# Part of the expert weights as plain float32, the rest split on VectorE alone, the gate inside a one-hot operand

## The chip, the cores and the metric

The kernel runs on one core of a Trainium2 chip, whose core has five engines: TensorE (PE, with its weight loads shown as PEld), VectorE (DVE), ScalarE (ACT), GpSimd (POOL) and SyncE (SP), which issues most of the transfers. The metric is the device time of one launch in microseconds, lower is better; it is taken as the median of several runs.

## What is computed

Two transformer blocks follow each other (256 tokens, width 1024, float32 throughout), then a third stage with a latent and a context stream in two layers. The change touches one thing alone, the expert layer of the latent stream, once in each of the two layers. For a token row `x` with norm and modulation already applied it is

```python
qry = (xb @ w_query).reshape(P, 8, 2, 128)
s = jnp.einsum('phcd,hckd->phck', qry, sub_keys)          # 128 keys for each half
top_s, top_i = lax.top_k(s, 16)
cand_s = top_s[..., 0, :, None] + top_s[..., 1, None, :]  # 16 x 16 pairs
cand_i = top_i[..., 0, :, None] * 128 + top_i[..., 1, None, :]
best_s, pos = lax.top_k(cand_s.reshape(...), 16)
idx = jnp.take_along_axis(cand_i.reshape(...), pos, axis=-1)
gate = jax.nn.softmax(best_s, axis=-1)
act = gelu(jnp.einsum('pd,phkd->phk', xb, u_tab[idx]))
out = jnp.einsum('phk,phkd->pd', gate * act, v_tab[idx])
```

There are 128 x 128 experts, so each of the two tables `u_tab` and `v_tab` has 16384 rows of 1024, and a token picks 8 x 16 of them.

## The kernel before

The latent stream's expert layer is done densely (`class Dense`, driven by `lat_peer`): instead of gathering rows, all 16384 experts are multiplied with all tokens, in 128 chunks of 128 experts, and the gates, which are zero for experts not picked, are multiplied in between. Layer 0 does all 256 tokens so (T = 256); in layer 1 the first 48 tokens go by gathers (`Few`) and 208 are dense (T = 208). A float32 product is made of three products in a reduced format, fp32r: `split` takes a weight tile of 128 x 512 (256 KB), casts it to its upper 12 bits `sh` (line 509 on VectorE, 511 on ScalarE), subtracts that from the tile to get the lower part `sl` (line 513, on VectorE or GpSimd), and the product is `sh*xh + sh*xl + sl*xh`, where `xh` and `xl` are the parts of the activation (`xs`, made once in `peer_in`). The pairs in the constants `SPD`, `SPT` and `SPL` say, for each tile in turn, whether VectorE casts, and whether VectorE subtracts: before, `SPT` and `SPD` (routing; second matrix) cast on ScalarE and subtract on GpSimd and VectorE by turns, and `SPL` (first matrix) does the even tiles on ScalarE and GpSimd and the odd ones on VectorE alone.

The stages of a layer, in order:

1. Routing (`prep`, `peer_route`, products by `lin_cols_split`, 16 blocks of the query weights), woven with the first chunks of the first matrix.
2. The first matrix, first 56 chunks (`up_first`): for each chunk two weight tiles `ut`, products into the PSUM bank `au`, then in layer 1 a sum `cf` (lines 1924 and 1925), then Gelu into `G`.
3. The spread (`up_spread`): for each four tokens (64 times in layer 0, 52 in layer 1) `spread` makes two one-hot operands, `ohl` over the first key (|iota - key| on ScalarE, line 1945, then Relu(1 - .), line 1946) and `ohr` over the second (an equality on VectorE, line 1947, times the gate on GpSimd, line 1949), multiplies them on TensorE into `gp`, and multiplies the result into `G` (line 1960) or copies it there (line 1962). One chunk of the first matrix goes with each spread. In `up`, the columns whose gates are already there take another product on GpSimd (line 1932).
4. The second matrix (`down`), in two halves of 512 columns, 128 chunks each: one tile `vt` a chunk, and `g`, the chunk of `G`, split into `gs` (line 1990 on ScalarE, 1991 on VectorE), products into four banks `y` that are summed over all chunks. Halves end in `finish`.

Beside all this runs another stream of work, the context's gathers (`gather_sum`: a row gather into `gv` issued on GpSimd, and a multiply-add on VectorE, 128 x 1024) and in layer 1 those of `Few`. `tick` issues a step of it after so many microseconds of TensorE's work, and places it behind the instruction `E.pin`, which `split` sets to the latest subtraction on GpSimd.

Weight tiles `ut`, `vt` and the query weights `w` come from one ring of five buffers (`UB = 5`, tag "w") and are all loaded by SyncE's queue, in the order of the program. `h` and `l` tiles have five buffers (`HB`, `VB`), `gs` four. A tile scheduler orders each engine's queue ahead of time; an engine does its queue in that order. A load waits until the last reader of the tile five before it is done:

## Time and profile before

| | |
|---|---|
| median of 3 runs | 4541.75 us (4533.81 to 4548.85) |
| span of the profiled execution | 4545.1 us, 3.35 above the median |
| granted TensorE clock, mean | 0.927 |
| busy: PE, DVE, ACT, POOL | 85%, 77%, 44%, 54% |

The stages that the change touches lie between 2309 and 3398 us (layer 0) and between 3554 and 4533 us (layer 1):

| stage | layer 0, us | length | layer 1, us | length |
|---|---|---|---|---|
| routing | 2309 to 2364 | 55 | 3554 to 3607 | 53 |
| first matrix, first 56 chunks (layer 1: 48) | 2364 to 2570 | 206 | 3607 to 3777 | 170 |
| spread, with about 63 chunks | 2570 to 2894 | 324 | 3777 to 4080 | 303 |
| last chunks of the first matrix | 2894 to 2926 | 32 | 4080 to 4142 | 62 |
| second matrix, half 0 | 2926 to 3152 | 226 | 4142 to 4344 | 202 |
| second matrix, half 1 | 3152 to 3398 | 246 | 4344 to 4533 | 189 |

Together they are 2068 us. "Busy" counts an engine's time inside instructions; for matmuls the ends are modelled, so that two that follow each other overlap, and the time of one is read from the distance between starts.

### The profile page before, as it was taken

How to read it: one execution, taken by the hardware profiler on the slowest of the kernel's cores; microseconds unless marked ns; L12 is line 12 of the kernel's file. 1: busy time of each engine (PE TensorE's matmuls, PEld its weight loads, DVE VectorE, ACT ScalarE, POOL GpSimd, SP SyncE). 2: the span in 40 equal slices, each digit the busy share in tenths (PEclk: the TensorE clock that was granted, in tenths of full speed). 3: DMA queues.
4: the chain of work that ended last, by engine and by line, in shares of the span. 5: the costliest groups of instructions: out<-in, count | busy, mean ns of one | idle time of the engine just before them, and what ended most of it. 6: DMA issues, size and time to landing. Idle time of an engine off the chain costs nothing.

```text
span 4545.1 us, 71987 instructions
## 1 busy us (share of the span) xinstructions
PE 3866.8 (85%) x24403; PEld 3111.8 (68%) x24403; DVE 3509.3 (77%) x6513; ACT 1982.2 (44%) x5025; POOL 2439.9 (54%) x2019
## 2 busy tenths in 40 slices
PE   7899878889998888897888887888887978777888
PEld 6756756377563676664588887777666777677878
DVE  4674576588565995775678899888877899998988
ACT  3224315345253443222443365455444445654555
POOL 1013235577544873113537688766554467787654
PEclk8998999999999999997899999999999988989999
DMA  5452627888878873447444754676762345557775
GB/s 173 127 187 63 235 83 267 305 288 284 304 266 296 286 257 126 123 153 240 145 150 144 244 172 159 196 229 226 247 222 68 125 144 183 181 172 231 262 234 194
DMA packets 384176, 907.74 MB, mean 200 GB/s; under 512 B 87888, under 2 KB 90000, under 8 KB 383040
## 3 DMA queue, kind: packets, MB, share of 16 engines
q1 hardware_dynamic: 270560, 553.05, 36.9%
q0 software_dynamic: 87552, 318.81, 21.2%
q10 hardware_dynamic: 25696, 31.28, 2.3%
q8 instruction: 193, 3.16, 0.3%
q14 instruction: 175, 1.43, 0.1%
HBM read 887.67 MB, written 15.32 MB: 199 GB/s over the span
## 4 chain that ended last, share of the span: by engine, by line
DVE 16%; PE 16%; DMA 7%; issue 6%; POOL 4%; ACT 1%; DVEq 0%; POOLq 0%; SPq 0%; ACTq 0%
PE y L392 8%; DVE sl L513 4%; PE au L392 3%; DMA gv<-in_peer_v_dram,ixz 2%; DVE gs L1991 2%; DVE sh L509 2%; DMA vt<-in_peer_v_dram 2%; POOL sl L513 2%; PE acs L392 2%; DMA ut<-in_peer_ut_dram 1%; DVE ohr L1947 1%; POOL ohr L1949 1%; DMA gv<-in_peer_v_dram,fix 1%; DVE G L1960 1%; DVE fg L1841 1%
## 5 line engine op out<-in xcount | busy, mean ns | idle before, releaser
L392 PE MATMUL au<-xs,sh 128*128 128x256 f32 (+1 forms) x3072 | 749.7, 329 | 73.1 <-DVE cf L1925 55.1
L392 PE MATMUL y<-gs,sh 128*128 128x512 f32 (+1 forms) x2048 | 710.1, 401 | 106.0 <-DVE gs L1991 95.8
L392 PE MATMUL au<-xs,sl 128*128 128x256 f32 (+1 forms) x2048 | 583.1, 288 | 58.5 <-DVE sl L513 39.8
L392 PEld LDWEIGHTS au<-xs,sh 128*128 128x128 f32 x3072 | 541.0, 202 | 88.4 <-DVE cf L1925 45.1
L392 PE MATMUL y<-gs,sl 128*128 128x256 f32 (+1 forms) x2048 | 554.4, 277 | 13.1 <-POOL sl L513 13.1
L513 POOL TENSOR_TENSOR sl<-vt,sh 128x512 fp32r<-128x512 f32 x256 | 388.2, 1519 | 262.6 <-ACT sh L511 221.1
L392 PEld LDWEIGHTS y<-gs,sh 128*128 128x128 f32 x2048 | 399.1, 196 | 183.7 <-DVE gs L1991 122.9
L392 PEld LDWEIGHTS au<-xs,sl 128*128 128x128 f32 x2048 | 417.9, 204 | 80.0 <-DVE sl L513 54.8
L511 ACT CAST sh<-vt 128x512 fp32r<-128x512 f32 x512 | 316.1, 619 | 347.7 <-PE y L392 165.1
L513 POOL TENSOR_TENSOR sl<-ut,sh 128x512 fp32r<-128x512 f32 x256 | 384.1, 1504 | 118.4 <-ACT sh L511 94.7
L1991 DVE TENSOR_TENSOR gs<-G,gs 128x256 fp32r<-128x256 f32 (+1 forms) x512 | 396.0, 790 | 39.3 <-ACT gs L1990 38.8
L1754 POOL DMA_INDIRECT gu<-in_peer_u_dram,ixs x256 | 289.8, 1132 | 248.8 <-DVE gu L1756 133.2
L392 PEld LDWEIGHTS y<-gs,sl 128*128 128x128 f32 x2048 | 401.5, 198 | 18.1 <-POOL sl L513 15.7
L1756 DVE SCALAR_TENSOR_TENSOR gu<-gu,h 128x1024 f32<-128x1024 f32 x256 | 361.8, 1420 | 63.7 <-DMA gu<-in_peer_u_dram,ixs 62.1
L392 PE MATMUL acs<-xs,sh 128*128 128x256 f32 (+1 forms) x1792 | 373.0, 304 | 27.5 <-ACT sh L511 15.0
L392 PE MATMUL acc<-hdn,w 128*128 128x256 f32 x1280 | 313.5, 398 | 33.3 <-DVE cvu L1269 12.6
L392 PEld LDWEIGHTS acs<-xs,sh 128*128 128x128 f32 x1792 | 299.2, 202 | 49.4 <-issue 18.6
L392 PE MATMUL acs<-xs,sl 128*128 128x256 f32 x960 | 285.3, 300 | 27.5 <-POOL sl L513 20.8
L513 DVE TENSOR_TENSOR sl<-ut,sh 128x512 fp32r<-128x512 f32 x256 | 289.7, 1133 | 15.7 <-ACT sh L511 1.6
L392 PEld LDWEIGHTS acc<-hdn,w 128*128 128x128 f32 x1280 | 245.9, 199 | 78.9 <-DVE cvu L1269 14.8
L1774 DVE SCALAR_TENSOR_TENSOR y<-gv,col,y 128x1024 f32<-128x1024 f32 x157 | 243.5, 1551 | 62.7 <-DMA gv<-in_peer_v_dram,ixz 50.1
L513 POOL TENSOR_TENSOR sl<-w,sh 128x512 fp32r<-128x512 f32 x140 | 193.3, 1384 | 143.2 <-ACT sh L511 124.0
(654 smaller groups left out, 8894.7 us busy)
## 6 DMA issues: line engine op xcount, KB each, us to landing
ut<-in_peer_ut_dram SPq DMA_DIRECT2D x512, 256.0 KB
vt<-in_peer_v_dram SPq DMA_DIRECT2D x512, 256.0 KB
w<-in_ada_w_dram SPq DMA_DIRECT2D x96, 512.0 KB
w<-in_dn_w_in_dram SPq DMA_DIRECT2D x96, 512.0 KB
w<-in_w_up_dram SPq DMA_DIRECT2D x88, 512.0 KB
wd<-in_w_down_dram SPq DMA_DIRECT2D x44, 512.0 KB
w<-in_w_in_dram SPq DMA_DIRECT2D x40, 512.0 KB
w<-in_dn_w_out_dram SPq DMA_DIRECT2D x32, 512.0 KB
```

The lines of the kernel that those rows point to most:

```text
L392: return E.nc.tensor.matmul(out, lhsT=lhsT, rhs=rhs, start=start, stop=stop)
L509: nc.vector.tensor_copy(h, src)
L511: nc.scalar.copy(h, src)
L513: ins = eng.tensor_tensor(out=l, in0=src, in1=h.bitcast(F32), op=ALU.subtract).ins
L1754: nc.gpsimd.indirect_dma_start(out=g, out_offset=None, in_=E.a["peer_u"], in_offset=bass.IndirectOffsetOnAxis(ap=ix[:, s, k:k + 1], axis=0))
L1756: nc.vector.scalar_tensor_tensor(out=g, in0=g, scalar=1.0, in1=h, op0=ALU.mult, op1=ALU.mult, accum_out=c[:, k:k + 1])
L1774: nc.vector.scalar_tensor_tensor(out=y, in0=g, scalar=c[:, k:k + 1], in1=y, op0=ALU.mult, op1=ALU.add)
L1841: nc.vector.scalar_tensor_tensor(out=g, in0=g, scalar=1.0, in1=h, op0=ALU.mult, op1=ALU.mult, accum_out=self.c[:, s, k:k + 1])
L1947: nc.vector.tensor_tensor(out=R, in0=self.iota[:, None, :].to_broadcast([128, 4, 128]), in1=col(0), op=ALU.is_equal)
L1949: nc.gpsimd.tensor_tensor(out=R, in0=R, in1=col(2), op=ALU.mult)
L1960: nc.vector.tensor_tensor(out=g[:, :, 0:m], in0=ph[:, :, 0:m], in1=g[:, :, 0:m], op=ALU.mult)
L1991: nc.vector.tensor_tensor(out=gs[:, 1], in0=g, in1=gs[:, 0].bitcast(F32), op=ALU.subtract)
```

## The change

- In both layers `SPD` is now one pair: every split tile is cast on ScalarE and subtracted on VectorE; GpSimd subtracts nothing there. `E.pin` is now the latest subtraction whichever engine does it.
- In the routing and the first matrix only the second half of the 1024 rows of the weights is split; the first half is multiplied as it is, a float32 tile times the float32 activation (`xf`), one product in place of three. `peer_in` keeps `hT` for it and splits only its second half. In `up` the split tile is loaded and multiplied first, the plain one last.
- In `down` every fourth chunk (`FD = 4`, c = 3, 7, ...) is plain: `vt` times `g` itself, without `gs`.
- The gate goes into `ohl`: in place of one Relu over 128 x 512 there are four over 128 x 128 with the gate as bias and its negative as scale (a fourth row of `sl`, made by one more ScalarE multiply). The multiply on GpSimd (line 1949) is gone.
- The multiply of `G` (line 1932) moves from GpSimd to VectorE.

Descriptions in the code's comments were taken out as well. The core of the diff, with function names in the place of line numbers:

```diff
@@ split
     eng = nc.vector if lo else nc.gpsimd
-    ins = eng.tensor_tensor(out=l, in0=src, in1=h.bitcast(F32), op=ALU.subtract).ins
-    if not lo:
-        E.pin = ins
+    E.pin = eng.tensor_tensor(out=l, in0=src, in1=h.bitcast(F32), op=ALU.subtract).ins
@@ lin_cols_split (xf: the plain activation, or None)
+    k0 = 4 if xf is not None else 0
...
-        for o in (0, 4):
+        for o in range(k0, 8, 4):
             h, l = split(E, P, ws[o // 4], o // 4)
...
+        for k in range(k0):
+            mm(E, p[:, 0:256], ws[0][:, k * 128:k * 128 + 128], xf[:, k], False, k == k0 - 1)
@@ Dense.__init__, Dense.prep
-        self.sl = P.tile([128, 3, 256], F32, name="sl")
+        self.sl = P.tile([128, 4, 256], F32, name="sl")
...
+                nc.scalar.mul(self.sl[:, 3, t * 128:t * 128 + 128], p[:, 256:384], -1.0)
@@ Dense.up
-        for o in (0, 4):
+        us = []
+        for o in (4, 0):
             ut = E.wp.tile([128, 512], F32, name="ut", tag="w")
             nc.sync.dma_start(ut, a["peer_ut"][self.i, c, :, o:o + 4].rearrange("p k e -> p (k e)"))
-            h, l = split(E, PU, ut, 2 * c + o // 4)
...
+            us.append(ut)
+        h, l = split(E, PU, us[0], 0)
+        for k in range(4):
+            e = slice(k * 128, k * 128 + 128)
+            x = self.xs[:, k, self.nb:self.nb + o1]
...
+        for k in range(4):
+            mm(E, p[:, 0:T], us[1][:, k * 128:k * 128 + 128], self.xf[:, k, self.nb:256], False, k == 3)
...
-            nc.gpsimd.tensor_tensor(out=g[:, 0:n], in0=g[:, 0:n], in1=cf[:, 0:n], op=ALU.mult)
+            nc.vector.tensor_tensor(out=g[:, 0:n], in0=g[:, 0:n], in1=cf[:, 0:n], op=ALU.mult)
@@ Dense.spread
-            nc.scalar.activation(L[:, j], self.iota, AF.Abs, bias=self.sl[:, 1, t + j:t + j + 1], scale=-1.0)
-        nc.scalar.activation(L, L, AF.Relu, scale=-1.0, bias=1.0)
-        nc.vector.tensor_tensor(out=R, in0=self.iota[:, None, :].to_broadcast([128, 4, 128]), in1=col(0),
-                                op=ALU.is_equal)
-        nc.gpsimd.tensor_tensor(out=R, in0=R, in1=col(2), op=ALU.mult)
+            nc.scalar.activation(L[:, j], self.iota, AF.Abs, bias=col(1, j), scale=-1.0)
+        for j in range(4):
+            nc.scalar.activation(L[:, j], L[:, j], AF.Relu, scale=col(3, j), bias=col(2, j))
+        nc.vector.tensor_tensor(out=R, in0=self.iota[:, None, :].to_broadcast([128, 4, 128]),
+                                in1=self.sl[:, 0, t:t + 4, None].to_broadcast([128, 4, 128]), op=ALU.is_equal)
@@ Dense.down
+            r = self.i * 16384 + c * 128
+            vt = E.wp.tile([128, 512], F32, name="vt", tag="w")
+            nc.sync.dma_start(vt, a["peer_v"][r:r + 128, n * 512:n * 512 + 512])
+            end = last and c == cs[-1]
+            if c % FD == FD - 1:
+                for k in range(4):
+                    mm(E, self.y[k][:, 0:T], vt[:, k * 128:k * 128 + 128], g, False, end)
+                continue
             gs = PV.tile([128, 2, T], F32R, name="gs", bufs=4)
@@ peer_in
-        hT = norm_T(E, PL, x, A, "hp", shift=B)
-        xs = split_x(E, P, hT, "xs", nb=nb)
+        hT = norm_T(E, P, x, A, "hp", shift=B)
+        xs = split_x(E, P, hT[:, 4:8], "xs", nb=nb)
@@ lat_peer
-                sp, E.sp = E.sp, SPT
+                E.sp = SPD
                 weave(M.prep(P, PU, nm), ups, *WP)
-                E.sp = sp
...
-                E.sp = SPD
                 M.down(PV, 0, range(128))
@@ constants
-SPD = ((0, 0), (0, 1))
-SPT = ((0, 0), (0, 1))
+SPD = ((0, 1),)
+FD = 4
```

What moves in the queues. First SyncE's queue about a third into half 0 of layer 0's second matrix: its rows are loads of `vt`, with the semaphores that each waits for (`Pool_`, `DVE_`, `PE_`: the last reader of the buffer's earlier tile). Before:

```order
L1994 DMA vt_26925<-in_peer_v_dram 128x512 [waits DMAHW1_49,Pool_49]
L1994 DMA vt_26942<-in_peer_v_dram 128x512 [waits DMAHW2_49,DVE_49]
L1994 DMA vt_26959<-in_peer_v_dram 128x512 [waits DMAHW3_49,Pool_49]
L1994 DMA vt_26979<-in_peer_v_dram 128x512 [waits DMAHW4_49,DVE_49]
L1994 DMA vt_26996<-in_peer_v_dram 128x512 [waits DMAHW5_49,Pool_49]
L1994 DMA vt_27013<-in_peer_v_dram 128x512 [waits DMAHW6_49,DVE_49]
```

and the changed kernel, at the same place:

```order
L2000 DMA vt_25239<-in_peer_v_dram 128x512 [waits DMAHW2_49,DVE_49]
L2000 DMA vt_25256<-in_peer_v_dram 128x512 [waits DMAHW3_49,DVE_49]
L2000 DMA vt_25273<-in_peer_v_dram 128x512 [waits DMAHW5_49,DMAHW0_49,DVE_49]
L2000 DMA vt_25282<-in_peer_v_dram 128x512 [waits PE_49]
L2000 DMA vt_25299<-in_peer_v_dram 128x512 [waits DMAHW6_49,DVE_49]
L2000 DMA vt_25316<-in_peer_v_dram 128x512 [waits DMAHW7_49,DVE_49]
L2000 DMA vt_25333<-in_peer_v_dram 128x512 [waits DMAHW4_49,DMAHW1_49,DVE_49]
L2000 DMA vt_25342<-in_peer_v_dram 128x512 [waits PE_49]
```

A load waited for GpSimd and VectorE by turns; now three wait for VectorE and every fourth for TensorE, which is the reader of a plain tile.

Second, VectorE's queue in the last chunks of layer 1's second matrix, where `sl` is a weight's lower part, `gs` that of `g`. Numbers rise in the order in which the program creates tiles: gs_43019 and vt_43022 before, vt_39229 and gs_39231 after, are of one chunk. Before:

```order
L513 TENSOR_TENSOR sl_43025<-vt_43022,sh_43024 128x512 [waits DMAHW1_49,PE_49,Activation_49]
L1991 TENSOR_TENSOR gs_43002<-G0_32357,gs_43002 128x208 [waits Activation_49]
L1991 TENSOR_TENSOR gs_43019<-G0_32357,gs_43019 128x208 [waits Activation_49]
L513 TENSOR_TENSOR sl_43059<-vt_43056,sh_43058 128x512 [waits DMAHW3_49,PE_49,Activation_49]
L1991 TENSOR_TENSOR gs_43036<-G0_32357,gs_43036 128x208 [waits Activation_49]
L1991 TENSOR_TENSOR gs_43053<-G0_32357,gs_43053 128x208 [waits Activation_49]
```

and the changed kernel:

```order
L513 TENSOR_TENSOR sl_39218<-vt_39212,sh_39217 128x512 [waits DMAHW5_49,PE_49,Activation_49]
L2008 TENSOR_TENSOR gs_39197<-G0_30035,gs_39197 128x208 [waits Activation_49]
L513 TENSOR_TENSOR sl_39235<-vt_39229,sh_39234 128x512 [waits DMAHW6_49,PE_49,Activation_49]
L2008 TENSOR_TENSOR gs_39214<-G0_30035,gs_39214 128x208 [waits Activation_49]
L513 TENSOR_TENSOR sl_39258<-vt_39252,sh_39257 128x512 [waits DMAHW0_49,PE_49,Activation_49]
L2008 TENSOR_TENSOR gs_39231<-G0_30035,gs_39231 128x208 [waits Activation_49]
L513 TENSOR_TENSOR sl_39275<-vt_39269,sh_39274 128x512 [waits DMAHW1_49,PE_49,Activation_49]
L2008 TENSOR_TENSOR gs_39254<-G0_30035,gs_39254 128x208 [waits Activation_49]
```

Before, one subtraction of a weight stands ahead of two of `g`. Now they alternate, and gs_39231, of the third split chunk of its group of four, stands behind sl_39258, of the first chunk of the next group; the tile of that one, vt_39252, is loaded into the buffer of the plain chunk of the group before.

Third, GpSimd's queue while the gates are spread, layer 0. Before:

```order
L1769 DMA gv_23612<-in_peer_v_dram,ixz_20755 128x1024
L1932 TENSOR_TENSOR G1_20760<-G1_20760,cf_23417 128x80
L1949 TENSOR_TENSOR ohr_23541<-ohr_23541,sl_18846 128x512
L513 TENSOR_TENSOR sl_23622<-ut_23619,sh_23621 128x512
L1932 TENSOR_TENSOR G1_20760<-G1_20760,cf_23475 128x84
L1949 TENSOR_TENSOR ohr_23599<-ohr_23599,sl_18846 128x512
L513 TENSOR_TENSOR sl_23680<-ut_23677,sh_23679 128x512
L1769 DMA gv_23713<-in_peer_v_dram,ixz_20755 128x1024
```

and the changed kernel, from the preparation of layer 0's expert layer on:

```order
L1884 IOTA iota 128x128
L1667 TENSOR_TENSOR cand<-v_18855 128x256 x8
L1694 TENSOR_TENSOR cand<-cand,fi 128x256 x16
L1667 TENSOR_TENSOR cand<-v_18856 128x256 x8
L1694 TENSOR_TENSOR cand<-cand,fi 128x256 x16
L1772 DMA gv<-in_peer_v_dram,ixz 128x1024 x121
```

The subtractions (line 513), the multiplies of `ohr` (1949) and of `G` (1932) are gone from between the gathers, and 121 gathers stand in a row.

## Rows read from the trace of the kernel before

**Rows 1.** The stretches that the change touches, cut at the stages of the two layers (the stage of each row is named in the table of times above): length, then busy time and count of each engine in the order PE, PEld, DVE, ACT, POOL, the granted TensorE clock as a share of full speed, the busy share of the DMA engines and GB/s. The line ahead gives the span.

```profile
core 0 of [0], span 4545.1 us
...
2309.00:2364.00 55.00, 54.17 (x439) 53.88 (x440) 42.30 (x191) 27.98 (x51) 29.95 (x24) 0.95 0.57 179
2364.00:2570.00 206.00, 179.12 (x1380) 171.87 (x1379) 180.38 (x395) 75.14 (x159) 139.89 (x120) 0.97 0.58 186
2570.00:2894.00 324.00, 267.78 (x2033) 254.65 (x2032) 310.02 (x346) 180.10 (x564) 277.35 (x226) 0.96 0.53 171
2894.00:2926.00 32.00, 27.32 (x203) 25.61 (x201) 25.14 (x23) 7.73 (x19) 21.46 (x22) 0.95 0.64 201
2926.00:3152.00 226.00, 194.41 (x1027) 162.63 (x1027) 197.73 (x233) 121.83 (x267) 147.61 (x102) 0.96 0.73 238
3152.00:3398.00 246.00, 206.27 (x1059) 169.72 (x1058) 202.24 (x231) 117.20 (x255) 145.33 (x109) 0.94 0.69 226
3554.00:3607.00 53.00, 52.48 (x303) 46.56 (x304) 41.00 (x160) 29.24 (x74) 23.16 (x20) 0.94 0.49 155
3607.00:3777.00 170.00, 139.99 (x792) 128.25 (x791) 167.80 (x450) 78.10 (x182) 105.06 (x94) 0.89 0.46 147
3777.00:4080.00 303.00, 237.84 (x1425) 224.62 (x1425) 284.97 (x411) 180.34 (x548) 237.28 (x203) 0.89 0.58 181
4080.00:4142.00 62.00, 45.14 (x277) 42.48 (x276) 53.65 (x71) 21.99 (x61) 49.60 (x46) 0.96 0.63 206
4142.00:4344.00 202.00, 173.96 (x1027) 161.80 (x1027) 188.43 (x235) 114.19 (x267) 134.91 (x101) 0.95 0.79 258
4344.00:4533.00 189.00, 170.83 (x1089) 165.41 (x1088) 161.49 (x214) 109.57 (x253) 103.12 (x79) 0.96 0.68 217
```

**Rows 2.** Part 5 of the page, two of its groups: the products of the first matrix with the high part of the weights, and those of the second; busy time, mean ns of one, and after the second bar the idle time of the engine ahead of them and what ended most of it.

```profile
L392 PE MATMUL au<-xs,sh 128*128 128x256 f32 (+1 forms) x3072 | 749.7, 329 | 73.1 <-DVE cf L1925 55.1
L392 PE MATMUL y<-gs,sh 128*128 128x512 f32 (+1 forms) x2048 | 710.1, 401 | 106.0 <-DVE gs L1991 95.8
```

**Rows 3.** The view by tile, VectorE alone, whole span: duration of one in ns, least, median and most. The subtraction of a split weight tile in the first and the second matrix, that of a split `g`, the comparison that makes `ohr`, and the multiply-add of a gather.

```profile
L513 DVE TENSOR_TENSOR sl<-ut,sh x256: 662/876/3727, 2361.3 to 4131.4; 128x512 fp32r<-128x512 f32 x128
L513 DVE TENSOR_TENSOR sl<-vt,sh x256: 675/680/2830, 2927.5 to 4527.7; 128x512 fp32r<-128x512 f32 x128
...
L1991 DVE TENSOR_TENSOR gs<-G,gs x512: 359/413/3391, 2925.4 to 4528.6; 128x256 fp32r<-128x256 f32 x86, 128x208 fp32r<-128x208 f32 x85
...
L1947 DVE TENSOR_TENSOR ohr<-iota,sl x116: 665/801/2516, 2426.5 to 4070.7; 128x512 f32<-128x512 f32 x116
...
L1774 DVE SCALAR_TENSOR_TENSOR y<-gv,col,y x157: 1267/1285/4598, 2121.5 to 3346.1; 128x1024 f32<-128x1024 f32 x157
```

**Rows 4.** The timeline in layer 0 while the gates are spread, 2600 to 2609 us: start, duration, engine, line, operation; of its rows a subtraction on GpSimd and one on VectorE, and the multiply into `G` a little later.

```profile
2599.49 1.45 POOL L513 TENSOR_TENSOR sl<-ut,sh 128x512 fp32r<-128x512 f32 x1
...
2599.91 1.57 DVE L513 TENSOR_TENSOR sl<-ut,sh 128x512 fp32r<-128x512 f32 x1
...
2601.41 0.71 DVE L1960 TENSOR_TENSOR G<-gp,G 128x248 f32<-128x248 f32 x1
```

**Rows 5.** The timeline of GpSimd and of VectorE, 2498 to 2499.3 us, layer 0, first matrix: the issue of a gather, and a subtraction inside it.

```profile
2498.20 0.95 POOL L1769 DMA_INDIRECT gv<-in_peer_v_dram,ixz  x1 [1.54 <-PE au L392]
...
2498.36 0.69 DVE L513 TENSOR_TENSOR sl<-ut,sh 128x512 fp32r<-128x512 f32 x1
```

**Rows 6.** The chain of waits, one step of it near the end of the span: start, length, what it was, how many. Each chunk has eight such products.

```profile
4467.56 44.53 PE y L392 x296
```

**Rows 7.** The timeline of TensorE alone, in four places: start, duration with the modelled end, operation and how many in a row. In order: products of a split tile in the first matrix; plain float32 products in an earlier block (16 records in a row, and the start of what follows); products of a split tile in the second matrix, layer 0; the eight passes of four one-hot products and the next product behind them.

```profile
2503.16 0.28 PE L392 MATMUL au<-xs,sl 128*128 128x256 f32 x1
...
2503.52 0.28 PE L392 MATMUL au<-xs,sl 128*128 128x256 f32 x1
...
1807.37 3.62 PE L392 MATMUL acc<-hdn,w 128*128 128x256 f32 x16
1810.83 0.27 PE L1285 MATMUL st<-cst,cvs 128*128 128x128 f32 x1
...
3002.18 0.40 PE L392 MATMUL y<-gs,sh 128*128 128x512 f32 x1
...
3002.53 0.39 PE L392 MATMUL y<-gs,sh 128*128 128x512 f32 x1
...
2585.39 1.05 PE L392 MATMUL gp<-ohr,ohl 128*128 128x128 f32 x8
2586.19 0.48 PE L392 MATMUL au<-xs,sh 128*128 128x256 f32 x2
```

**Rows 8.** Groups of instructions by line and shape, ScalarE, 2580 to 2890 us: busy time and mean ns of one, then idle time ahead.

```profile
L1945 ACT ACTIVATE ohl<-iota,sl 128x128 f32<-128x128 f32 x240 | 76.8, 406 | 0.1
L1946 ACT ACTIVATE ohl<-ohl 128x512 f32<-128x512 f32 x60 | 38.6, 643 | 0.0
L511 ACT CAST sh<-ut 128x512 fp32r<-128x512 f32 x60 | 36.6, 609 | 1.9 <-PE au L392 1.9
```

**Rows 9.** The waits of SyncE's queue of transfers, whole span: at which line, for whose instruction, us in total, times, longest.

```profile
SPq L1994 <- POOL sl L513: 267.6, 168, 9.2
```

**Rows 10.** The chain of waits, two steps that are weight loads: start (when SyncE issued it) and time until it had landed.

```profile
2481.52 2.60 DMA ut<-in_peer_ut_dram
...
4147.99 4.43 DMA vt<-in_peer_v_dram
```

46 lines of the change are left out of this document (21 added, 25 removed).

## The prediction, as it went on record

> **What bounds the kernel now.** I read the stretches of the two layers first [rows 1], then the costliest groups for who waits [rows 2], then single instructions. The touched stretches are 2068 us of the execution's 4545.1, and 2477 us are left alone. No engine is full in them: TensorE is busy 1749 us of 2068, VectorE 1855, GpSimd 1415, ScalarE 1063 (sums over the twelve rows). VectorE is nearest, and where the gates are spread it and GpSimd are both long: 310 and 277 of 324 us. But VectorE is not long by its own work. A subtraction of a weight tile takes it 0.66 us at least and 0.88 in the median in the first matrix, up to 3.7; that of `g` 0.36 to 3.4, `ohr` 0.67 to 2.5 [rows 3]. The timeline says when: with GpSimd's subtraction beside it VectorE's takes 1.57 us [rows 4], with a gather's issue around all of it 0.69 [rows 5]. So GpSimd's arithmetic, not its gathers, stretches VectorE. TensorE waits for what VectorE delivers: in the second matrix 106 us ahead of the first products, nearly all for `gs`, in the first 73 us, 55 of them for `cf` [rows 2]. When nothing is in the way it needs no more than its own work: near the end 296 products, 37 chunks, pass in 44.5 us, 1.20 a chunk [rows 6], where layer 1's half 0 spends 202/128 = 1.58 [rows 1].
>
> The Trainium skill (SBUF — State Buffer, "Who interferes with whom") says the same of the two engines: a VectorE instruction with two SBUF inputs collides with a GpSimd one that reads SBUF, and one is held for the other's whole length. The 1.57 us agrees; the issue of a gather would by that rule collide only if it read SBUF through that port, and the 0.69 shows no collision.
>
> **TensorE's own work grows.** Split tile in the first matrix, T = 256: three products, 0.36 us from one `sl` product to the next, for each 128 rows; plain: 3.46/16 = 0.216 a record from the start at 1807.37 to the next row's, and a product is two records, so 0.43 [rows 7]. Four of eight row blocks change, +0.29 a chunk: 2.88 to 3.17. For T = 208 I scale by columns: 2.40 to 2.60. Second matrix, a split pair takes 0.35 [rows 7], a chunk 1.40, a plain one 1.73; a group of four 5.6 becomes 5.9, and 4.8 becomes 5.0 in layer 1. Over 128 chunks of each first matrix (37 + 26), 64 groups of each second (21 + 13) and the routing (9) that is +106 us of TensorE work; it is paid in full where TensorE is the limit.
>
> **VectorE and GpSimd lose.** GpSimd's 512 subtractions, its 116 `ohr` and its `G` multiplies go. VectorE does one subtraction of 0.68 for a chunk of the first matrix where it did a cast and a subtraction, each stretched, and one for three of four chunks of the second. It gains the `G` multiply, about 0.36 by the shortest `gs` of like size [rows 3]. Per chunk with a spread in layer 0: 0.68 + 0.36 + `ohr` 0.67 + `G` 0.71 [rows 4] + six tenths of a gather's multiply-add of 1.27 [rows 3] = 3.2 us. ScalarE: the four Abs take 0.32 each in busy time, a Relu of four times the size 0.64 [rows 8]; four short Relus at the Abs' price are 1.28, so +0.64 for 116 spreads. That gives 218 us over 62 chunks in layer 0, 3.5 a chunk. No engine passes TensorE (3.17 + 0.80 for the eight passes of the one-hot products [rows 7] = 3.97).
>
> **A new wait.** Before, the buffer of a weight tile came free with the subtraction, and SyncE never waited for TensorE in these layers but for VectorE and GpSimd [rows 9]. A plain tile is read by TensorE itself. Every fourth load of the second matrix and every second one of the first now waits for that, and all later loads queue behind it on SyncE. With five buffers the plain tile of chunk c is followed in its buffer by chunk c+5, the first of the next group but one. So a loop closes: end of the plain chunk, load, cast, subtraction, products, end of the next. What it costs hangs on how long a load takes to land. On the chain one takes 2.60 and one 4.43 us [rows 10], but a chain picks the late ones. I take 2.8, near the shorter, since fewer loads are under way when each waits for its buffer.
>
> In most groups the second split chunk's `gs` stands behind the subtractions of its own group and one multiply-add of a gather, and the loop spans two groups. Layer 1: 0.2 to issue, 2.8, cast 0.61 [rows 8], three subtractions 2.04, multiply-add 1.27, `gs` 0.36, handing over 0.1 = 7.4, then the second and third chunk and the plain one 1.2 + 1.2 + 1.4 = 3.8; (7.4 + 3.8)/2 = 5.6 a group. Layer 0 with its longer `gs`: (7.8 + 4.53)/2 = 6.17. In 50 of 127 groups (12 and 12 in layer 0, 6 and 20 in layer 1, counted in VectorE's queue) the third split chunk's `gs` is queued behind the `sl` of the next group's first tile, the row pair shown for layer 1's end. There the loop is within one group: 0.2 + 2.8 + 0.61 + 0.68 + 0.41 + 0.1 = 4.8, then the third chunk 1.40 and the plain one 1.73: 7.9 us a group (7.35 in layer 1), against 4 x 1.77 = 7.1 (6.3) before. So these groups get slower. The 0.1 and 0.2 are estimates.
>
> **The sum, stage by stage** (before, then after, us):
> - Routing 55 to 62 and 53 to 62: a block of plain and split halves waits by the same loop, since the plain half of the next block but one is loaded when this one's products end: 0.2 + 2.8 + 0.61 + 0.68 + 0.1 = 4.4, (4.4 + 3.17)/2 = 3.8, 16 blocks.
> - First chunks: TensorE's busy 179 + 16 = 195 from 206; layer 1 140 + 10 = 150 from 170, where VectorE, 168 busy, loses its stretches.
> - Spread: from 324 to 270, 62 chunks of 4.35, a tenth over 3.97, since the Relus queue behind casts that wait for loads; layer 1 303 to 240 (3.8 a chunk; TensorE 2.6 + 0.66, ScalarE (180 + 52 x 0.64)/63 = 3.4). The bounds are 246 and 286 in layer 0 (pitches; busy time plus 18), 206 and 251 in layer 1.
> - Last chunks 32 to 29 and 62 to 54.
> - Second matrix: layer 0 half 0, 12 x 7.9 + 20 x 6.17 = 218 from 226; half 1 the same with the 20 us that it has over half 0 now, 238 from 246 (240 taken); layer 1 half 0, 6 x 7.35 + 26 x 5.6 = 190 from 202 (191), half 1, 20 x 7.35 + 12 x 5.6 = 214 and some for its end, 218 from 189.
>
> That is 1929 for 2068, -139: 4406 on the execution's scale. It stood 3.35 above the median, so **4403 us**.
>
> **Rivals.** (A) The loop doesn't bind, since loads land sooner or the queue runs ahead. Then stages go by TensorE's work and a twentieth: a second-matrix half is 198 in layer 0 and 168 in layer 1, the routing 52, the spread 255 and 230: some 155 us less, **4250**. For it: the 1.20 us a chunk at the end of before [rows 6]. Against: the loop's waits are written in SyncE's queue. The Trainium skill (DMA: Bandwidth & Descriptors, "Specifications") gives 0.6 us to the first byte and about 358 GB/s, which for 256 KB is an estimate of 1.3 us to land. By it each loop would be 1.5 us shorter and this rival true; the trace's 2.60 speaks against it [rows 10].
>
> (B) Slower than before: the load loops, with landing 4.5 us in place of 2.8, as the chain's 4.43 [rows 10]. One us more of landing costs a bad group 1 us (50), another half (77, so 38), a routing block half (32, so 16), a chunk with a spread about a third (40 us): 145. At 4.5 that is +246, **4650**; from 3.75 on the change is a loss. For it: DMA engines are already busy 73 and 79% of the time in both half 0 [rows 1], and the gathers, freed from GpSimd's queue, may bunch up. Against: the same bytes as before, in fewer loads at a time.
>
> (C) The collisions stay, because gathers are still issued on GpSimd while VectorE works. Then only the `ohr` waits go and TensorE's extra work eats half: about **4500**. Against: 0.69 inside a gather's issue [rows 5].
>
> **How the numbers follow.** The forecast's case, 4340 to 4480, has 0.6; A 0.2, B 0.12, C 0.06. What a run of this kernel can tell from no change is about 0.3%, 14 us. The forecast's case, A and nearly all of C are faster, B is slower: faster 0.83, within 0.3% 0.05, slower 0.12. For 8 in 10 the range leaves out B and the farther side of A: 4270 to 4520.
>
> **What would show it.** In the profile after, `sl` on VectorE at 0.68 in the median with few beyond 1 us, and `gs` at 0.41 and 0.36, show the collisions gone; else C. SyncE waiting for TensorE (`y`, `au`) at the loads' lines, and TensorE idle ahead of `y` for VectorE's `gs` in groups of 7 to 8 us at layer 1's end, show the loop; if chunks pass there at 1.25, A. Layer 1's half 1 is the one stage that should be longer than before; if all four halves are, B. The spread stages should carry most of the gain, 117 of 139 us. The forecast fails most easily on the landing time, by 145 us for each microsecond.

## The result, and the profile after

The changed kernel takes 4341.97 us in the median of 4 runs (4337.04 to 4349.55), the kernel before in the same runs 4537.78: ratio 0.9567, 95% interval 0.9542 to 0.9592. It is 196 us faster. The forecast was 4403, 139 us faster; the time lies inside the range, 61 us below the forecast on the side of rival A (4250), and just inside the forecast's own case (4340 to 4480).

The profiled execution has a span of 4335.2 us. Cut at the same stages as before, by TensorE's first product of each, the touched stretches of the changed kernel are these (the columns as in [rows 1]; the first six rows are layer 0, in the order routing, first 56 chunks, spread, last chunks, half 0, half 1; then layer 1):

```profile
2301.40:2362.60 61.20, 59.65 (x373) 55.11 (x374) 39.58 (x177) 15.92 (x31) 3.11 (x5) 0.96 0.44 143
2362.60:2561.20 198.60, 186.67 (x1151) 171.13 (x1150) 136.85 (x373) 66.67 (x146) 59.83 (x64) 0.98 0.62 200
2561.20:2823.30 262.10, 259.98 (x1783) 246.06 (x1781) 198.99 (x348) 239.86 (x752) 38.12 (x41) 0.99 0.67 211
2823.30:2853.00 29.70, 27.54 (x170) 24.57 (x169) 12.07 (x22) 7.55 (x19) 3.15 (x4) 1.00 0.67 209
2853.00:3058.70 205.70, 195.15 (x1027) 166.89 (x1027) 142.80 (x237) 91.43 (x203) 41.93 (x35) 0.99 0.82 262
3058.70:3290.10 231.40, 216.52 (x1087) 178.32 (x1086) 145.43 (x235) 92.20 (x205) 53.09 (x47) 0.97 0.69 226
3433.90:3489.20 55.30, 55.30 (x305) 49.21 (x305) 39.01 (x174) 19.36 (x56) 2.72 (x5) 1.00 0.48 148
3489.20:3641.80 152.60, 137.45 (x809) 131.98 (x807) 123.81 (x408) 76.35 (x189) 40.30 (x44) 0.97 0.53 166
3641.80:3899.00 257.20, 228.17 (x1426) 217.50 (x1424) 181.33 (x401) 218.30 (x684) 40.18 (x41) 0.98 0.69 218
3899.00:3946.20 47.20, 43.38 (x256) 41.31 (x256) 31.50 (x71) 21.23 (x57) 7.89 (x9) 1.00 0.83 262
3946.20:4135.00 188.80, 169.55 (x1025) 161.16 (x1026) 135.76 (x238) 87.03 (x200) 39.05 (x35) 0.99 0.85 277
4135.00:4322.60 187.60, 174.89 (x1087) 167.80 (x1088) 107.88 (x208) 80.07 (x189) 17.69 (x15) 0.99 0.65 209
```

They sum to 1877 us, where 2068 stood before and 1929 was forecast. The other 20 us of the span lie outside these stretches, 13 of them between the layers: 143.8 us pass there now and 156.5 before, but that stretch takes 144 to 155 us in the variants of the changed kernel below, nearly all with the same code there, so this part can't be put down to the change. In layer 1 "first chunks" and "spread" are cut near chunks 48 and 112 in both kernels.

| stage, us | layer 0: before | forecast | after | layer 1: before | forecast | after |
|---|---|---|---|---|---|---|
| routing | 55 | 62 | 61 | 53 | 62 | 55 |
| first chunks | 206 | 195 | 199 | 170 | 150 | 153 |
| spread | 324 | 270 | 262 | 303 | 240 | 257 |
| last chunks | 32 | 29 | 30 | 62 | 54 | 47 |
| half 0 | 226 | 218 | 206 | 202 | 191 | 189 |
| half 1 | 246 | 240 | 231 | 189 | 218 | 188 |

VectorE alone, by tile, over the whole span (ns: least, median, most), beside [rows 3]:

```profile
L513 DVE TENSOR_TENSOR sl<-vt,sh x384: 677/692/3559, 2853.0 to 4316.0; 128x512 fp32r<-128x512 f32 x192
L513 DVE TENSOR_TENSOR sl<-ut,sh x256: 658/693/1225, 2358.6 to 3939.8; 128x512 fp32r<-128x512 f32 x128
...
L2008 DVE TENSOR_TENSOR gs<-G,gs x384: 359/392/570, 2852.4 to 4316.9; 128x256 fp32r<-128x256 f32 x96, 128x208 fp32r<-128x208 f32 x96
...
L1957 DVE TENSOR_TENSOR ohr<-iota,sl x116: 658/685/712, 2418.9 to 3889.4; 128x512 f32<-128x512 f32 x116
```

The reader is to see the middle and last numbers: `sl` in the first matrix 876 to 693 in the median and 3727 to 1225 at most, `gs` 3391 to 570 at most, `ohr` 801 to 685 and 2516 to 712. Gathers are still issued on GpSimd all the while. What still stretches VectorE is what arithmetic is left on GpSimd: three subtractions of `vt` take more than 1 us (3559 ns is one of them) and six of `ut`, and each of the nine lies beside a GpSimd TENSOR_TENSOR of the routing or of the context's stream. In the kernel before, the subtractions of `ut` sorted by what GpSimd did meanwhile give the same answer: 0.68 us in the median beside an idle GpSimd (45 of them), 0.69 beside the issue of a gather alone (34), 1.34 beside arithmetic (177). VectorE's busy time in the touched stretches falls from 1855 to 1295 us, GpSimd's from 1415 to 347, while TensorE's stays (1749, 1754).

That TensorE's busy time stays although it has more to do goes with its clock, a term that the forecast left out. The granted clock was 0.89 to 0.97 in these stretches before [rows 1] and is 0.96 to 1.00 now. It has two levels, 2.4 and 1.2 GHz; by the means of the rows, some 245 of the 2068 us were spent at the lower one before, and some 63 of the 1877 now (an estimate: twice the length times what the clock lacks to 1). Lowest it was in layer 1's first chunks and spread, 0.89, where TensorE was busy 140 of 170 and 238 of 303 us; now it is 0.97 and 0.98 there, with TensorE busy 137 of 153 and 228 of 257. Busy time times clock gives about 1650 us of work before and 1725 after. No run here holds the clock fixed, so what it gave back is not told apart from the waits that went.

Two groups of the page, the first beside [rows 2]:

```profile
L392 PE MATMUL y<-gs,sh 128*128 128x512 f32 (+1 forms) x1536 | 537.2, 404 | 46.7 <-DVE gs L2008 39.9
...
L511 ACT CAST sh<-vt 128x512 fp32r<-128x512 f32 x384 | 236.6, 619 | 409.3 <-DMA vt<-in_peer_v_dram 347.2
```

TensorE's idle time ahead of these products is 46.7 us where it was 106.0, and 39.9 of it is for `gs` where it was 95.8. And a new wait stands one step earlier: ScalarE's casts of `vt` stand idle for 347 us in all for the landing of a load. Whether that costs anything is what the runs below settle.

### The profile page after: what moved, and what is told of

It is laid out like the page before. It is cut to its first block, busy times and chain, and to the rows that moved or that the text cites. A ratio compares the mean times of both kernels' runs of the same rounds, so it can differ in the third digit from the quotient of the medians.

```text
span 4335.2 us, 68372 instructions
## 1 busy us (share of the span) xinstructions
PE 3866.4 (89%) x23827; PEld 3109.4 (72%) x23827; DVE 2945.9 (68%) x6431; ACT 1930.5 (45%) x5045; POOL 1366.8 (32%) x1209
## 4 chain that ended last, share of the span: by engine, by line
PE 24%; DMA 16%; DVE 13%; ACT 4%; issue 4%; POOL 2%; SPq 0%; ACTq 0%; DVEq 0%; POOLq 0%
DMA vt<-in_peer_v_dram 8%; PE au L392 7%; PE y L392 6%; PE acc L392 4%; DMA ut<-in_peer_ut_dram 4%; DVE sl L513 3%; ACT sh L511 2%; PE acs L392 2%; PE gp L392 2%; DMA gv<-in_peer_v_dram,ixz 1%; POOL cand L1694 1%; DMA w<-in_peer_wq_dram 1%; DVE y L1777 1%; DVE tmp L1388 1%; DVE gu L1759 1%
## 5 line engine op out<-in xcount | busy, mean ns | idle before, releaser
L392 PE MATMUL y<-gs,sh 128*128 128x512 f32 (+1 forms) x1536 | 537.2, 404 | 46.7 <-DVE gs L2008 39.9
L392 PE MATMUL au<-hp,ut 128*128 128x256 f32 (+1 forms) x2048 | 455.1, 365 | 1.1 <-DMA ut<-in_peer_ut_dram 1.1
L513 DVE TENSOR_TENSOR sl<-vt,sh 128x512 fp32r<-128x512 f32 x384 | 270.5, 710 | 239.6 <-ACT sh L511 232.6
L392 PE MATMUL y<-gs,sl 128*128 128x256 f32 (+1 forms) x1536 | 402.0, 272 | 4.6 <-DVE sl L513 4.3
L392 PE MATMUL au<-xs,sh 128*128 128x256 f32 (+1 forms) x1536 | 388.9, 333 | 16.3 <-DVE cf L1934 15.1
L392 PEld LDWEIGHTS au<-hp,ut 128*128 128x128 f32 x2048 | 364.4, 193 | 22.6 <-DMA ut<-in_peer_ut_dram 1.6
L1772 POOL DMA_INDIRECT gv<-in_peer_v_dram,ixz x128 | 138.3, 1081 | 611.5 <-DVE y L1777 553.4
L392 PE MATMUL au<-xs,sl 128*128 128x256 f32 (+1 forms) x1024 | 285.9, 279 | 23.2 <-DVE sl L513 23.1
L392 PEld LDWEIGHTS au<-xs,sh 128*128 128x128 f32 x1536 | 262.5, 192 | 29.0 <-DVE cf L1934 19.2
L511 ACT CAST sh<-ut 128x512 fp32r<-128x512 f32 x256 | 158.8, 620 | 253.5 <-DMA ut<-in_peer_ut_dram 244.9
```

The lines of the kernel that those rows point to most:

```text
L392: return E.nc.tensor.matmul(out, lhsT=lhsT, rhs=rhs, start=start, stop=stop)
L511: nc.scalar.copy(h, src)
L513: E.pin = eng.tensor_tensor(out=l, in0=src, in1=h.bitcast(F32), op=ALU.subtract).ins
L1772: nc.gpsimd.indirect_dma_start(out=g, out_offset=None, in_=E.a["peer_v"], in_offset=bass.IndirectOffsetOnAxis(ap=ix[:, k:k + 1], axis=0))
```

## The experiments

All are variants of the changed kernel or of the kernel before, timed against the kernel before on the same chip. Stage lengths come from each run's trace, cut as above. The ratio to compare with is the changed kernel's 0.9567.

**1. GpSimd's arithmetic brought back, without its results.** Two GpSimd subtractions on a tile of their own for each split chunk of both matrices:

```diff
+        self.dm = P.tile([128, 256], F32, name="dm")
+        E.nc.gpsimd.memset(self.dm, 0.0)
...
+        for _ in range(2):
+            nc.gpsimd.tensor_tensor(out=self.dm, in0=self.dm, in1=self.dm, op=ALU.subtract)
         h, l = split(E, PU, us[0], 0)
...
```

> The changed kernel with two GpSimd subtractions of 128x256 added to every split chunk of both matrices, on a tile that nothing else reads: 640 chunks, about 2 x 0.65 us each. Nobody waits for them, so they add collisions alone. Theory (GpSimd's arithmetic stretched VectorE, and that was the loss): VectorE's subtraction of a weight rises from 0.69 in the median to 0.9 or more with many above 1.2, that of g likewise, and the time rises from 4342 by 60 to 150 us. Rival (collisions are harmless; before, products waited for the results of the slow GpSimd subtractions): the durations rise but the time stays within 20 us of 4342.

Measured: 4483.72 us, ratio 0.9879 (0.9834 to 0.9923), 142 us above the changed kernel. The spread stages take 303 and 288 us (262 and 257), half 0 of both layers 220 and 214 (206 and 189), the rest a few us more. By tile, VectorE:

```profile
L513 DVE TENSOR_TENSOR sl<-vt,sh x384: 673/693/3059, 2912.3 to 4456.5; 128x512 fp32r<-128x512 f32 x192
L513 DVE TENSOR_TENSOR sl<-ut,sh x256: 661/866/1255, 2365.0 to 4054.2; 128x512 fp32r<-128x512 f32 x128
...
L1961 DVE TENSOR_TENSOR ohr<-iota,sl x116: 667/788/1127, 2429.6 to 3998.2; 128x512 f32<-128x512 f32 x116
```

`sl` in the first matrix has 866 again, `ohr` 788: nearly before's 876 and 801, with nothing waiting for what GpSimd makes. In the second matrix the median stays (693, not the 0.9 us expected), but 122 of the 384 take more than 1 us, where three did. GpSimd is busy 1410 us in the touched stretches, as before (1415), and VectorE needs 1558 us for the work that takes it 1295 in the changed kernel. So the theory holds, with one reserve: GpSimd also issues the gathers, and they now queue behind the added instructions. In 2565 to 2815 us VectorE's multiply-adds of the gathers are

```profile
L1777 DVE SCALAR_TENSOR_TENSOR y<-gv,col,y 128x1024 f32<-128x1024 f32 x34 | 51.8, 1523 | 36.4 <-DMA gv<-in_peer_v_dram,ixz 36.4
```

that is, 36.4 of 250 us idle for a gather's landing, which the changed kernel doesn't have there. GpSimd's arithmetic costs in two ways, by stretching VectorE and by holding up the queue of gathers; this run doesn't divide the 142 us between them.

**2. Every other subtraction on GpSimd again.**

```diff
-SPD = ((0, 1),)
+SPD = ((0, 0), (0, 1))
...
-        h, l = split(E, PU, us[0], 0)
+        h, l = split(E, PU, us[0], c)
...
-            h, l = split(E, PV, vt, c)
+            h, l = split(E, PV, vt, c - c // 4)
```

> The changed kernel with every other split tile subtracted on GpSimd again, in both matrices; the rest of the change stays. It brings back collisions and the waits for GpSimd's results, at half of before's count. Theory (moving the subtractions to VectorE carries most of the gain): 60 to 130 us above 4342, most of it in the spread stages and the second matrix. Rival (the plain tiles carry it, by sparing split work): less than 25 us.

Measured: 4482.24 us, 0.9871 (0.9828 to 0.9914), 140 us above: the theory, a little beyond its upper end (130). The four halves take 230, 253, 216 and 196 us, 81 more than in the changed kernel, the spread stages 280 and 270, 31 more.

**3. The other way round: before, with that part alone.** All split tiles cast on ScalarE and subtracted on VectorE, nothing else changed.

```diff
-    ins = eng.tensor_tensor(out=l, in0=src, in1=h.bitcast(F32), op=ALU.subtract).ins
-    if not lo:
-        E.pin = ins
+    E.pin = eng.tensor_tensor(out=l, in0=src, in1=h.bitcast(F32), op=ALU.subtract).ins
...
-                E.sp = sp
...
-SPD = ((0, 0), (0, 1))
-SPT = ((0, 0), (0, 1))
+SPD = ((0, 1),)
+SPT = ((0, 1),)
```

> The kernel before, with one part of the change alone: every split tile cast on ScalarE and subtracted on VectorE, in routing and both matrices; no plain tiles, gate and G multiplies still on GpSimd. Theory (taking the subtractions off GpSimd carries most of the gain): 4380 to 4440, and the second matrix near 187, 217, 182 and 168 us as in the run without plain chunks. Rival (without plain tiles VectorE and ScalarE are overloaded in the first matrix): above 4480.

Measured: 4308.53 us, 0.9496 (0.9453 to 0.9539). This one part brings 231 us, more than the whole change. The halves take 187, 219, 184 and 168 us, first chunks 182 and 138, routing 55 and 52, spread 293 and 286. In the first matrix this also moves half of the casts from VectorE to ScalarE; in the second matrix, where all casts were on ScalarE before, it moves the subtraction alone, and the four halves there take 758 us for 863, 105 of the 231. All else in the change together costs some 34 us, and outside the spread it brings nothing in any stage and costs in nearly all. The next three runs take these other parts one by one out of the changed kernel.

**4. No plain chunk in the second matrix.**

```diff
-FD = 4
+FD = 1000
```

> The changed kernel with no plain chunk in the second matrix: all 512 are cast on ScalarE and subtracted on VectorE. TensorE does 34 us less. If the prediction's loop through the plain chunk (load only after TensorE's last product of it) held the four halves back, they fall from 206, 232, 189 and 188 us to near 8 us over TensorE's 180 and 154 each: 30 to 60 us faster. Rival (VectorE, with 0.69 + 0.39 us for each chunk and the gathers' multiply-adds, or the landing of loads in a ring of five, is the limit): no gain or up to 40 us slower.

Measured: 4304.04 us, 0.947 (0.9426 to 0.9513), 38 us faster than with plain chunks; halves 187, 217, 182 and 168, 61 us less than the changed kernel's 206, 231, 189 and 188 (the stretch between the layers and the start of the stages took 20 us more). VectorE, with a third more to subtract (512 tiles for 384), is not the limit. TensorE's saved work, 34 us by the forecast's prices, doesn't cover the 61; the plain chunks cost waits as well.

**5. No plain half in the first matrix and the routing.** `up` and `lin_cols_split` as before, but on ScalarE and VectorE.

```diff
...
-        for o in (4, 0):
+        for o in (0, 4):
...
-            us.append(ut)
-        h, l = split(E, PU, us[0], 0)
...
+            h, l = split(E, PU, ut, 2 * c + o // 4)
...
```

> The changed kernel with both halves of the first matrix and of the routing split again, on ScalarE and VectorE. TensorE does 72 us less, ScalarE one cast of 0.62 us more for each chunk, VectorE one subtraction of 0.69. Theory (ScalarE, busy 240 of 262 and 218 of 257 us, is at its limit in the spread stages): routing and first chunks 10 to 25 us shorter together, the spread stages 20 to 40 us longer each, in all 10 to 50 us above 4342. Rival (TensorE limits there): 50 to 70 us below 4342.

Measured: 4371.97 us, 0.9631 (0.9594 to 0.9668), 30 us slower. Routing 54 and 51 (61 and 55) and first chunks 184 and 138 (199 and 153) are 41 us shorter together: there TensorE pays for the plain half in full. The spread stages are 273 and 303 (262 and 257), 57 us longer: there the plain half spares ScalarE a cast and VectorE a subtraction. Without it ScalarE is busy 260 of 273 us in layer 0, ahead of TensorE (253), and 267 of 303 in layer 1, where no engine is full; that ScalarE holds the stage is shown, by experiment 12, only for layer 1 with plain halves.

**6. The gate on GpSimd again**, with one wide Relu.

```diff
-        for j in range(4):
-            nc.scalar.activation(L[:, j], L[:, j], AF.Relu, scale=col(3, j), bias=col(2, j))
+        nc.scalar.activation(L, L, AF.Relu, scale=-1.0, bias=1.0)
...
+        nc.gpsimd.tensor_tensor(out=R, in0=R, in1=col(2), op=ALU.mult)
```

> The changed kernel with the gate multiplied into ohr on GpSimd again and one wide Relu for the four. ScalarE saves about 0.8 us for each of 116 spreads, GpSimd adds 1.05 us to the chain ahead of the one-hot products. Theory (GpSimd's arithmetic beside VectorE and in the chain costs more than ScalarE's time): spread stages 10 to 30 us longer each. Rival (ScalarE is the limit in layer 1's spread): that stage 10 to 25 us shorter, layer 0's the same.

Measured: 4364.02 us, 0.9604 (0.9569 to 0.9639), 22 us slower. Layer 0's spread goes from 262 to 297 us, layer 1's from 257 to 250. Each theory has the direction of one layer, and neither the size (35 us more for 10 to 30, 7 less for 10 to 25): in layer 0 GpSimd's multiply is the dearer, in layer 1 ScalarE's Relus are, and why the layers differ stays open. The Relus cost more than forecast. ScalarE in the changed kernel, 2565 to 2815 us (busy time, mean ns):

```profile
L1956 ACT ACTIVATE ohl<-ohl,sl 128x128 f32<-128x128 f32 x241 | 107.6, 497 | 0.0
L1954 ACT ACTIVATE ohl<-iota,sl 128x128 f32<-128x128 f32 x244 | 78.3, 406 | 0.1
```

The Relu with its own scale and bias for each partition takes 107.6/241 = 0.45 us of busy time, the Abs 0.32, which was the price forecast for both.

**7. Own buffers for the plain tiles** of the second matrix, three, beside the ring of five (split parts: four buffers for five).

```diff
+            if c % FD == FD - 1:
+                vt = PV.tile([128, 512], F32, name="vt", tag="vp", bufs=3)
+            else:
+                vt = E.wp.tile([128, 512], F32, name="vt", tag="w")
```

> The changed kernel with three buffers for the plain tiles of the second matrix alone, so that the ring of five serves split tiles alone; to make room the split parts have four buffers for five. If the loads are what the second matrix waits for (the ring is too short for a landing of 3.7 us, whoever frees a buffer), groups of four at layer 1's end fall from 5.7 to 6.0 us to about 5.1, and the four halves together by 25 to 50 us. If the transfers themselves are the limit (DMA engines busy 82 and 85 percent in both first halves), it changes less than 10 us.

Measured: 4274.37 us, 0.9409 (0.9366 to 0.9452), 68 us faster; halves 193, 208, 164 and 169, 80 us less together. That is more than the 25 to 50 us expected, and the transfers are not the limit. But the run changes two things, more buffers and a ring without plain tiles, so:

**8. A ring of seven**, shared as before (split parts: three buffers in the first matrix, four in the second; with five in the second there is no room, 32 KB a partition where 31.1 are left).

```diff
-UB, HB, VB, OB, N0, GB = 5, 5, 5, 2, 56, 2
+UB, HB, VB, OB, N0, GB = 7, 3, 4, 2, 56, 2
```

> The changed kernel with seven buffers for five in the shared ring of weight tiles; split parts have three buffers in the first matrix and four in the second to make room. Theory (the ring is too short for the landing time, whoever holds a buffer): the four halves fall from 206, 232, 189, 188 us to about those with own buffers for the plain tiles, 193, 208, 164, 169, and the whole to 4265 to 4300. Rival (a plain tile in the shared ring is what hurts, and own buffers cured that): halves within 15 us in all of the changed kernel's, 4325 to 4345.

Measured: 4235.56 us, 0.9344 (0.9322 to 0.9367), 106 us faster than the changed kernel and 30 below the range expected. The windows of the four halves (columns as above):

```profile
2852.00:3044.00 192.00, 190.28 (x1026) 165.76 (x1027) 141.41 (x236) 92.71 (x202) 47.82 (x35) 1.00 0.84 277
3044.00:3257.10 213.10, 204.43 (x1071) 174.14 (x1071) 141.31 (x229) 89.73 (x194) 57.18 (x46) 0.98 0.72 245
3892.50:4061.60 169.10, 162.69 (x1026) 161.20 (x1027) 133.75 (x240) 87.09 (x203) 53.05 (x35) 0.98 0.90 309
4061.60:4230.80 169.20, 169.20 (x1087) 168.38 (x1087) 110.26 (x207) 82.06 (x186) 18.38 (x15) 0.99 0.70 229
```

192, 213, 169 and 169 us, as with own buffers, with TensorE busy in 727 of 743 us; first chunks 193 and 143, spread 258 and 244, routing 59 and 54. Length alone does it in the halves (70 us less), though the DMA engines are then 84 and 90% busy in the first halves; the other stages, which the expectation left as they were, give 39 us more.

**9. The ring of seven without plain chunks in the second matrix** (`FD = 1000` in addition).

> The same ring of seven, with no plain chunk in the second matrix. If the ring was also what held the run without plain chunks (187, 217, 182, 168 us for TensorE's 180 and 154 a half), the halves fall to about 182, 205, 162 and 163 us and the whole to 4255 to 4275, as far as three buffers for the split parts do not hurt the first matrix. If VectorE is the limit there (0.69 + 0.39 us a chunk and the gathers), they stay within 10 us of 755 in all.

Measured: 4235.15 us, 0.9353 (0.9328 to 0.9378): no difference to the run with plain chunks. Halves 183, 214, 170 and 169 for 192, 213, 169 and 169. In the four halves together that is 737 us for 743, between the 712 expected and the rival's 755: of the gain over the ring of five without plain chunks (753 us), only 16 us came. So in a longer ring plain chunks cost nothing and bring nothing; what they cost in a ring of five was buffers.

**10. The kernel before in a ring of seven**, the same line of constants.

> The kernel before with the ring of seven (split parts: three buffers in the first matrix, four in the second). Theory (before, the second matrix was held by GpSimd's arithmetic, by collision and by its results, not by the loads): the four halves, 226, 246, 202 and 189 us, fall by less than 25 us in all; the first matrix may lose some 10 to 30 us a stage for lack of buffers for split parts. Rival (the ring was too short before as well): the halves fall by 45 us or more.

Measured: 4555.07 us, 1.0023 (1.0001 to 1.0045). Halves 211, 243, 203 and 183, 23 us less in all, and the first chunks 229 and 184 (206 and 170) most likely for want of buffers for split parts, of which experiment 11 shows the same. Before, the loads were not what held the second matrix. They became so with the plain chunks: without these a ring of seven saves 16 us in the halves (753 to 737), with them 70 (813 to 743).

**11. Plain tiles only where ScalarE is the limit.** Routing, first chunks and second matrix all split, plain halves from the spread on; three buffers for the split parts in the first matrix.

```diff
+        if n == 0 or n > self.T:
+            for o in (0, 4):
+                ut = E.wp.tile([128, 512], F32, name="ut", tag="w")
...
+        else:
+            us = []
...
```

> The changed kernel with plain tiles only where ScalarE is the limit: the first half of the rows of the first matrix in chunks that go with a spread or come behind; routing, the first chunks and the second matrix all split. Ring of five; three buffers for the split parts in the first matrix. By the stages of the single runs: routing 54 and 51 us, first chunks about 183 and 138, spread 260 and 257, second matrix 187, 217, 182 and 168: 4240 to 4265. If three buffers are too few for two split tiles a chunk, the first chunks stay near 195 and 150 and it is 4280 or more.

Measured: 4306.88 us, 0.9505 (0.9473 to 0.9538). The first chunks took 213 and 180 us, not 183 and 138: with two split tiles a chunk three buffers for the split parts are too few, as the second theory had it (with five of them and the same code there, experiment 5 has 184 and 138). Routing came at 53 and 53, the spread at 257 and 248, the halves at 188, 219, 180 and 173. The loss of buffers hides what the plain tiles do, so this run says nothing on the change.

**12. Part of the one-hot operand on VectorE**, on top of the ring of seven.

```diff
-        for j in range(4):
+        na = 2 if self.nb else 3
+        for j in range(na, 4):
+            nc.vector.tensor_scalar(L[:, j], self.iota, col(1, j), col(2, j), op0=ALU.is_equal, op1=ALU.mult)
+        for j in range(na):
             nc.scalar.activation(L[:, j], self.iota, AF.Abs, bias=col(1, j), scale=-1.0)
-        for j in range(4):
+        for j in range(na):
             nc.scalar.activation(L[:, j], L[:, j], AF.Relu, scale=col(3, j), bias=col(2, j))
...
```

> The ring of seven of the changed kernel, plain tiles as in the change, and part of the one-hot operand ohl made on VectorE: for one of four tokens in layer 0 and two of four in layer 1 one instruction (equal to the key, times the gate) takes the place of the Abs and the Relu on ScalarE. If ScalarE is the limit in layer 1's spread (218 of 257 us busy in the changed kernel), that stage falls from 244 to 220 to 232 us and layer 0's, where TensorE is full, stays at 258: 4210 to 4228. If VectorE's queue delays the one-hot products instead, it stays at 4235 or above.

Measured: 4210.45 us, 0.9267 (0.9232 to 0.9302), the fastest of all. Layer 1's spread, its window:

```profile
3648.30:3868.80 220.50, 213.11 (x1378) 207.87 (x1378) 198.97 (x489) 150.37 (x459) 41.68 (x40) 0.99 0.77 248
```

220.5 us for 244, with ScalarE busy 150 and TensorE 213: TensorE is the limit now, as it is in layer 0 (258.5). The one VectorE instruction that does the work of two on ScalarE (0.32 + 0.45 us of busy time) is cheap (VectorE, 3650 to 3865 us):

```profile
L1955 DVE TENSOR_SCALAR ohl<-iota,sl 128x128 f32<-128x128 f32 x82 | 25.5, 360 | 0.0
```

25.5/82 = 0.31 us each.

## Why the forecast held, and where it was off

**Collisions: right, and larger than the rest.** The first step, that GpSimd's arithmetic and not its gathers stretches VectorE, is shown from both sides: durations fall to near their least values with the gathers still there, go back up with arithmetic that nobody waits for (experiment 1), and this part alone makes the kernel before 231 us faster (experiment 3), 105 of them in the second matrix, where it moves the subtraction and nothing else. Rival C is out. Not divided is how much of that was stretching, how much was gathers and results that queued on GpSimd, and how much came back through TensorE's clock.

**TensorE's extra work: right.** The forecast had +106 us, paid where TensorE is the limit. TensorE is busy 94 us longer than in experiment 3's kernel, which has no plain tiles (1754, 1660), and where nothing waits a chunk of the first matrix takes 3.16 us (from one plain half at 2493.29 us to the next at 2496.45) for 3.17. In routing and first chunks TensorE was the limit: 41 us came back without plain halves (experiment 5), for a forecast share of 35 there. In the spread the extra work was not paid, and the plain halves won 57 us, most likely through ScalarE.

**The load loop: the wrong loop, too dear.** The step that was wrong is "there the loop is within one group: [...] 7.9 us a group (7.35 in layer 1)", the price of the bad groups, and with it "layer 1's half 1 is the one stage that should be longer". That stage came at 188 us where 218 was forecast, the largest miss of all, and half 0 of layer 0 at 206 for 218. The chain of waits of the changed kernel over one group near the end of layer 1 (start, length, what) shows what closes instead:

```profile
4262.94 3.69 DMA vt<-in_peer_v_dram
4266.63 0.02 issue
4266.65 0.02 ACTq L511
4266.67 0.04 issue
4266.71 0.63 ACT sh L511
4267.34 0.02 issue
4267.36 0.33 DVE sl L513
4267.69 0.28 issue
4267.97 0.37 DVE gs L2008
4268.34 0.32 DVE sl L513
4268.66 0.28 issue
4268.94 0.11 DVE gs L2008
4269.05 3.51 DMA vt<-in_peer_v_dram
```

From load to load it is 6.1 us: landing 3.69, cast 0.63, two subtractions of a weight and one of `g` between them 1.7, and then the next load, which has waited for VectorE's subtraction to give its buffer back. No product of TensorE is in it. The waits of SyncE's queue at the loads of the second matrix say the same (us, times, longest):

```profile
SPq L2000 <- DVE gs L2008: 214.7, 152, 5.8
...
SPq L2000 <- DVE sl L513: 188.9, 197, 6.5
SPq L2000 <- DMA vt<-in_peer_v_dram: 181.0, 128, 4.1
...
SPq L2000 <- PE y L392: 30.3, 47, 4.1
```

585 us for VectorE and landings, 30 for TensorE. (In the first matrix SyncE does wait for TensorE, 169 us in 110 loads, but 116 of them in layer 0's spread, where TensorE is the limit itself.) I had taken it that the plain tile's buffer goes to the first tile of the next group but one, and put TensorE's remaining 1.2 + 1.4 us into the loop. Near the end of layer 1 it goes to the second tile of a later group, and TensorE is through with it long before: in the timeline the plain chunk's products end at 4264.9 us, and the load that takes its buffer leaves at 4269.43, 0.38 us after the one queued ahead of it, which waited for VectorE. The landing, forecast at 2.8 us, was 3.7 here, so the loop's largest term was too small by 0.9 us, VectorE's part by 0.5, and its closing term too large by 2.6. (The 7.8 us of layer 0's longer loop are also 0.4 more than its terms give, 7.4 with a `gs` of 0.41.)

Over the whole run the landings were longer still. The profile's page gives their medians, in us, as far as it can tell them:

```profile
ut<-in_peer_ut_dram SPq DMA_DIRECT2D x512, 256.0 KB, 3.4
vt<-in_peer_v_dram SPq DMA_DIRECT2D x512, 256.0 KB, 4.3
```

By the forecast's own price, 88 us in the second matrix for each microsecond of landing, 4.3 us in place of 2.8 would have cost the halves some 130 us; they came out 54 us below the forecast (813 for 867), for the loop that carried this price hardly ever closed. What the loop that does close costs is the difference to a ring of seven: 813 us less 743 in the four halves, 70 us, and it hangs on the number of buffers. It came with the plain chunks, for without them the difference is 16 us (experiments 4 and 9), and 23 in the kernel before (experiment 10). So the forecast had the right culprit, a tile that gives its buffer back only when TensorE has read it, and the wrong way of paying. The rows near the end of layer 1 show the way: the plain tile loaded at 4262.05 us is multiplied from 4269.68 and done at 4270.96, so it keeps its buffer 9 us, where the split tile loaded behind it at 4262.94 gives its own back at 4268.05, after 5. And a buffer that the plain chunk gave back at 4264.9 stays empty for 4.5 us, since SyncE issues its loads in order. The ring of five is then a ring of fewer.

**Rival A** had the right end and the wrong reason. Its 4250 us, stages at TensorE's work and a little, is what a longer ring gives (4236), not shorter landings: in the ring of seven the page still gives 4.1 us for `vt`. The landing of 3.7 us in the chain above is further from the 1.3 us estimated from the Trainium skill (DMA: Bandwidth & Descriptors, "Specifications") than 2.60 was. **Rival B** is out, though its condition nearly came true: it had 4.5 us of landing and a loss from 3.75 on, and the median for `vt` was 4.3, but the halves were shorter or equal in all four places.

**ScalarE: underpriced.** "Four short Relus at the Abs' price" was 0.32 each and is 0.45, so ScalarE was busy 218 us in layer 1's spread for a forecast of 213 at a stage of 240, and 240 in layer 0's for 218. In layer 0 TensorE was the limit anyway (260 of 262 us). In layer 1 ScalarE held the stage at 257 for 240, as experiment 12 shows by taking its work away, 244 to 220.5. Its busy time was only 5 us above the forecast there, so most of the 17 us lies in how its work queued, which no run takes apart.

The sum was off by 52 us in the stages, of which 30 are layer 1's half 1 and 21 the halves of layer 0, less 17 for layer 1's spread; the rest are small. That the total came inside the range owes something to luck: in the halves a loop that hardly closes stood in for a wait on buffers, and the clock was not in the sum. The change was the sum of one good part, one that is good in one place and bad in another, and one that cost buffers.

## What to carry to other kernels

Price the parts of a change one by one: here one of them was worth more than the whole. Where a change lets a slower or later reader hold a loaded tile, count how long the tile keeps its buffer: with landing times of 3 to 5 us and loads that are issued in order, each only when its buffer is given back, one tile kept for 9 us shortens the ring for all, and two more buffers cured it here. And trace a suspected loop through the actual queue, from the row that waits to the row that it waits for, before pricing it: that a buffer is read by TensorE did not mean that its next load waited for TensorE.
